# A hybrid decoder step on one core: every SBUF row set to begin at a multiple of 256 bytes

## The chip, the core and the metric

The kernel runs on 1 core of one Trainium2 chip. The metric is the device time of one execution in microseconds, as a median over runs. A core has four computing engines with their own instruction queues (TensorE, called PE; VectorE, DVE; ScalarE, ACT; GpSimd, POOL), a fifth queue that mostly issues transfers (SyncE, SP), and 16 DMA engines. Its working memory, SBUF, has 128 partitions, and a "row" below is a stretch of consecutive bytes within one partition.

## The reference

One inference step of one decoder layer, for a prompt of 1,024 tokens and for 8 samples of 4 tokens (32 columns), in float32. Cut to what matters:

```python
h, gate = adaln_in(x, c, w_ada, b_ada, g_norm)       # RMS norm, scaled and shifted by a projection of c
(mq, mk, mv, mi, mf, mo, mz, aq, ak, av, az, gm, ga) = split_in(h @ w_in)
y_m, C, n, m = mlstm_branch(...)                     # 4 heads of 128, in chunks of 128 tokens, with a carried state
o = attn_prompt(q, k, v, sinks)                      # 8 query heads of 64, window 128, a sink per head
y_a = o * silu(az)
u = sigmoid(gm) * (y_m @ w_mo) + sigmoid(ga) * (y_a @ w_ao)
x = x + gate * (u @ w_o)
y = rmsnorm(x, g_final)
```

Outputs are y for prompt and samples, the mLSTM state, and the keys and values that are kept.

## The kernel before

**Layout.** Activations lie transposed: a partition is a channel (modulo 128), a column a token. T = 1,056 columns are the 1,024 prompt tokens and the 32 sample columns. Every float32 operand of a large product is split into two float32r tiles, a rounded high part and the remainder; a product is the sum of three matmuls, high by high, high weight by low moving, low weight by high moving. In the names, `h_h` and `h_l` are the two parts of h, and `wh_...` and `wl_...` those of the weights. In the trace's `out<-moving,weight` the moving operand comes first.

**Memory.** SBUF tiles come from two pools, `cp` for constants (each tile for the whole kernel) and then `sp` for working tiles. In `sp` each tag has a fixed number of slots, and a new tile of a tag takes a slot that an earlier one has left; whoever first writes it waits for the last reader of the earlier one. The tags that matter:

- `half` (helper `ht`): 50 slots of 128x512 float32, 2,048 bytes a partition. Nearly everything passes through it: raw x, attention units (`uqv`, `ukv`, `p`), mLSTM loads (`hq`, `hk`, `hv`, `et`, `qw`), gates (`gt`, `tga`), sums for a Strassen scheme (`t2h0` and so on) and the split output weights (`wo_...`).
- `wr` (9 slots), `wh` and `wl` (4 each): weights of 128x4x128, also 2,048 bytes.
- `h0`, `h1`, `l0`, `l1`: one slot each, the four large tiles. Each holds four rows of T columns (4,224 bytes): `h_h0` has channels blocks 0 to 3 of the high part, `h_h1` 4 to 7, `h_l0` and `h_l1` the remainders. Before that the same slots hold weights (`early_...`), later the high and low parts of the mLSTM output (`ym_h0`, `ym_l0`), the merged branches (`u_h1`, `u_l1`) and output rows (`rows_h`, `rows_l`).

As the built program places them, the pools' first tile begins at byte 1,152. The first `half` slot begins at byte 16,928, the `wr` slots at 119,328, `h0` at 137,760, `h1` at 154,656, `l1` at 171,552, `wh` at 188,704, `wl` at 196,896 and `l0` at 205,088. All of these leave the remainder 32 when divided by 256. A row of a large tile is 16.5 times 256 bytes, so its rows 0 and 2 leave the remainder 32 too, and its rows 1 and 3 the remainder 160.

**Stages.** Condition projections and the norm of x (about 0 to 65 us); the first projections `g_ak`, `g_av`, then `g_aq`, `g_mq`, `g_mk`, `g_mv` in pieces of 384, 384 and 288 columns that read rows of `h_h` and `h_l` (to about 215 us); 18 pairs of projections by a Strassen scheme (`block_products`: seven products `bx`, `bw`, `by`, `bz` of 12 matmuls of 512 columns per pair), of which four read rows of the large tiles (b11, b21, b22, t1) and three read sums in `half` slots (t2, t3, t4) (to about 650 us); the attention output by the same scheme; the mLSTM output (`g_w_mo`, pieces of 384, 384 and 288 columns that read rows of `ym`); the output product (`foX`, `foW`, `foY`, `foZ`) whose operands all lie in `half`, `wr`, `wh` and `wl` slots, and the final norm.

**Order.** PE's instructions stand in the order in which they are written out; a planner (`Side`) drops attention units, mLSTM head stages and the output-weight preparation (`out_weights`) between them by estimated times. In the middle of the kernel DVE, ACT and SP are ordered by the framework's scheduler, which knows the slots. A weight is split (`split_ahead`, a cast on ACT and a subtraction on DVE) two products before its use.

Of the kernel before, what the change touches and what calls it, by code (L numbers as in the profile page):

```python
# [10 lines left out]
F32 = mybir.dt.float32  # L11
F32R = mybir.dt.float32r
# [11 lines left out]
NT = 4  # L24
NS = NB * NT
T = SEQ + NS
NH = 4
PAST = 8192
WIN = 128
# [5 lines left out]

C_ID, C_S9, C_TRI, C_CM, C_AM, C_TS, C_CS, C_RS, C_S32, C_BM, C_S64 = 0, 128, 137, 265, 393, 649, 681, 713, 745, 777, 785
C_END = 849


def shape_constants():  # L40
    f = np.float32
    c = np.zeros((128, C_END), f)
    i = np.arange(128)
# [8 lines left out]
    c[:NS, C_CS:C_CS + NS] = np.where(ok, 0, NEG)  # L52
    c[:NH, C_RS:C_RS + NS] = np.where(s % NT == 0, NEG, 0)[None]
    for r in range(9):
# [9 lines left out]
    cs, sn = np.cos(ang).astype(f), np.sin(ang).astype(f)  # L64
    rope = np.zeros((128, 2, T), f)
    rope[:, 0] = 1
# [15 lines left out]
def job_columns():  # L82
# [5 lines left out]
    for g in range(4):  # L88
        cols["aq", g] = aq + pair(g)
        cols["az", g] = az + pair(g)  # L90
    for h in range(NH):
        for n, s in (("mq", mq), ("mk", mk), ("mv", mv), ("mo", mo), ("mz", mz)):
# [80 lines left out]
def body(tc, a):  # L173
    nc = tc.nc
    with ExitStack() as ctx:
        cp = ctx.enter_context(tc.tile_pool(name="cp", bufs=1))
        sp = ctx.enter_context(tc.tile_pool(name="sp", bufs=1))
# [3 lines left out]
        def pg(shape, name):  # L181
            return ps.tile(shape, F32, tag="g", bufs=2, name=name)
# [8 lines left out]
            return ps.tile(shape, F32, tag="o", bufs=2, name=name)  # L191

        def ht(shape, name, dt=F32):
            return sp.tile(shape, dt, tag="half", bufs=50, name=name)

        def sm(shape, name, bufs=3, dt=F32):
            return sp.tile(shape, dt, tag=name, bufs=bufs, name=name)
# [43 lines left out]
        def dma(out, in_, late=False):  # L241
            stores(in_.tensor)
            issue(out, in_, late)
# [52 lines left out]
        def load_x(p, k0, k1, ts):  # L296
            for k in range(k0, k1):
                ts.append(ht([128, 512], f"x{p}_{k}"))
                dma(ts[-1], a["xT"][:, p, k])
# [4 lines left out]
        issue(small, a["small"])  # L304
        load_x(0, 2, KT, xT[0])
        load_x(1, 0, KT, xT[1])
        cst = cp.tile([128, C_END], F32, name="cst")
        vec = cp.tile([128, 28], F32, name="vec")
        cT, xS = (small[:, o:o + KT * n].rearrange("p (k n) -> p k n", k=KT) for o, n in ((C_TRI + 28, 9), (C_TRI + 28 + KT * 9, NS)))
# [21 lines left out]
        def quarter(x, shape, name, dt=F32):  # L331
            return sp.tile(shape, dt, tag=x, bufs=1, name=f"{name}_{x}")
# [46 lines left out]

        hD = dp.tile([128, KT, T], F32, name="hD")  # L380
        PARTS = (0, 512), (512, 512), (SEQ, NS)
# [143 lines left out]
        hs = {}  # L525

        def h_hi(k, c0, n, x="h"):
            ks = k
            if isinstance(k, slice):
                k, ks = k.start, slice(k.start % 4, (k.stop - 1) % 4 + 1)  # L530
            q = f"{x}{k // 4}"
            if q not in hs:
                hs[q] = quarter(q, [128, 4, T], "h", F32R)
            return hs[q][:, k % 4 if k is ks else ks, c0:c0 + n]

        h_lo = lambda k, c0, n: h_hi(k, c0, n, "l")
# [58 lines left out]
        def gates(gp, zg, bias):  # L595
# [43 lines left out]
            nm, wi = gt2[:, 0], gt2[:, 1]  # L639
            aTs = cp.tile([NH, NS], F32, name="aTs")  # L640
            bTs = cp.tile([NH, NS], F32, name="bTs")
            V.tensor_copy(aT, tp[:32, 0])
# [56 lines left out]

            m0 = cp.tile([NH, NB], F32, name="m0")  # L700
            dma(m0, a["m0T"])
            cms = cp.tile([NH, NS], F32, name="cms")
            V.tensor_tensor_scan(cms, cst[:NH, C_RS:C_RS + NS], aTs, NEG, ALU.add, ALU.max)
# [107 lines left out]
        osm = cp.tile([128, NH, NS], F32, name="osm")  # L811
        yaD = [dp.tile([128, T], F32, name=f"yaD{g}") for g in range(4)]

# [157 lines left out]
        yhD = [dp.tile([128, SEQ], F32, name=f"yhD{h}") for h in range(NH)]  # L971
        ymD = [dp.tile([128, T], F32, name=f"ymD{h}") for h in range(NH)]
        qs = cp.tile([128, NH, NS], F32, name="qs")
# [274 lines left out]
        def split(src, his, los, cols, k, eng=V):  # L1248
            for i, c in enumerate(cols):
                raw = ht([128, 512], "yr")[:, :c.stop - c.start]  # L1250
                dma(raw, src[k][:, c])
                hi, lo = his(k, c.start, c.stop - c.start), los(k, c.start, c.stop - c.start)
                S.copy(hi, raw)
                eng.tensor_tensor(lo, raw, hi.bitcast(F32), op=ALU.subtract)

        PCOLS = [slice(c0, c0 + n) for c0, n in PIECES]
        HALF = slice(0, 512), slice(512, SEQ)
        taD, tmD = ([dp.tile([128, T], F32, name=f"{n}{d}") for d in range(KT)] for n in ("taD", "tmD"))

# [313 lines left out]
        ut, ymt = [], []  # L1573
        u = lambda k, c0, n: ut[k // 4][:, k % 4, c0:c0 + n]
# [96 lines left out]
        def att_products():  # L1671
            jobs = [AttPair(i) for i in range(4)]
            flat = [(0, 1)]
            for n in range(4):
                flat += [(n, i) for i in (5, 6, 2, 7)] + ([(n + 1, 1)] if n < 3 else []) + [(n, 3), (n, 4)]

            def split_ahead(j):
                if j < len(flat):
                    jobs[flat[j][0]].split(flat[j][1])

            yield
            ymt.extend(quarter(x, [128, 4, T], "ym", F32R) for x in ("l0", "h0"))
            yield
            jobs[0].load()
            for k in range(4):
                dma(c32[:, k], yaD[k][:, SEQ:T])
            yield
            jobs[0].gates()
            yield
            yield  # L1690
            jobs[0].split(1)
            jobs[0].samples()
            jobs[0].first_sums()
            yield
            jobs[0].split(5)
            yield
            ut.extend(quarter(x, [128, 4, T], "u") for x in ("h1", "l1"))
            for j, (n, i) in enumerate(flat):
                job_ = jobs[n]
                nxt = jobs[n + 1] if n < 3 else None  # L1700
                if i == 1 and nxt:
                    nxt.load()
                if i == 6:
                    if nxt:
                        nxt.gates()
                    if n in (0, 1, 3):
                        split(ymD, *ymx, PCOLS, {0: 2, 1: 3, 3: 1}[n], G if n == 3 else V)
                if i == 3 and n == 2:
                    split(ymD, *ymx, PCOLS, 0)
                if i == 2 and not nxt:  # L1710
                    for d in range(2):
                        preload(("w_mo", d))
                split_ahead(j + 2)
                if i == 3 and not nxt:
                    prefetch(("w_mo", 0))
                    gated(("w_mo", 0))
                if i == 1:
                    o = NX = pg([128, 512], "ax")
                elif i == 5:
                    o = Z = pa([128, 512], "az")  # L1720
                else:
                    o = {2: lambda: X, 3: lambda: W, 4: lambda: Y, 6: lambda: W, 7: lambda: Y}[i]()
                new = i in (1, 5)
                wh, wl = job_.w.pop(i)
                for k in range(2):
                    side.until(lambda: k in ya[OPERANDS[i]])
                    bh, bl = ya[OPERANDS[i]][k]
                    mm(o, wh[:, k], bh, start=(new and k == 0), stop=False, more=not new)
                    mm(o, wh[:, k], bl, start=False, stop=False, more=not new)
                    mm(o, wl[:, k], bh, start=False, stop=(k == 1), more=not new)  # L1730
                    side.tick()

                def copy_of(pool, name, src):
                    t = pool([128, 512], name)
                    if n == 0 and (j == 0 or i == 6):
                        mm(t, job_.g["A"][0][:, 0], ya["b11"][0][0], start=True, stop=True)
                    S.copy(t, src)
                    return t

                if i == 6:  # L1740
                    Y = copy_of(pa, "ay", W)
                    job_.samples_end()
                elif i == 2:
                    job_.done(0, 0, X)
                    if nxt:
                        nxt.samples()
                        nxt.first_sums()
                elif i == 5:
                    p5 = ht([128, 512], "p5")
                    S.copy(p5, Z)  # L1750
                elif i == 7:
                    job_.done(1, 1, p5, Y)
                elif i == 3:
                    job_.done(0, 1, p5, W)
                elif i == 4:
                    job_.done(1, 0, Y)
                if j == 0 or (i == 3 and nxt):
                    X = NX
                    W = copy_of(pg, "aw", X)
# [421 lines left out]
        for i, r in enumerate(blocks_of_rows):  # L2181
# [65 lines left out]
            else:  # L2247
# [9 lines left out]
                for f, (y, (c0, n)) in enumerate(zip(Y, parts)):  # L2257
# [3 lines left out]
                    if f:  # L2261
                        V.tensor_tensor(xb[1][:, hi], xb[1][:, hi], gf[:, hi], op=ALU.mult)
                        half = norm_sum(ss[:, 2:4], 1, 2)
# [82 lines left out]
```

## Time and profile before

| | |
|---|---|
| median of 3 runs | 842.34 us (842.21 to 842.41) |
| the profiled execution: its time | 842.49 us |
| its span, first to last instruction | 840.7 us |
| granted TensorE clock, mean | 0.997 |
| PE busy | 819.6 us (97%), 5,129 matmuls |
| DVE busy | 599.2 us (71%) |
| ACT busy | 421.7 us (50%) |
| POOL busy | 66.2 us (8%) |
| moved by DMA | 153.96 MB, 183 GB/s over the span |

Times inside the span count from its start. Matmuls overlap, so the length of one matmul in the trace is more than what it adds; what it adds is read from start to start. A line of the chain of waits such as `12.3 2.77 PE by L258 x12` says that twelve matmuls in a row took 2.77 us of the path that ended last. All recorded operations of DVE and ACT carry line 219 and all matmuls line 258, those of helpers.

### The profile page before, as it was taken

Reading aid. Unit: us, or ns where it says so; the run is one execution under the profiler, and the core shown is the slowest. Engines: PE = TensorE matmul, PEld = TensorE weight load, DVE = VectorE, ACT = ScalarE, POOL = GpSimd, SP = SyncE. Lnnn points to the kernel's source line nnn. Section 1 sums busy time; section 2 is a strip of 40 time slices with the busy share of each in tenths; the row PEclk is TensorE's granted clock in tenths of the full one; section 3 lists DMA queues with packets and bytes.
Section 4 is the critical chain, followed back from the end, with each engine's and each line's share of the span. In section 5 each row is a group of like instructions: output and inputs, shape, how many; then the busy total and the mean of one; then the engine's idle time right before and its main releaser. Section 6 shows DMA issues by size and latency. Waiting matters only on the chain.

```text
span 840.7 us, 15062 instructions
## 1 busy us (share of the span) xinstructions
PE 819.6 (97%) x5129; PEld 666.8 (79%) x5129; DVE 599.2 (71%) x1501; ACT 421.7 (50%) x1032; POOL 66.2 (8%) x128
## 2 busy tenths in 40 slices
PE   6999999999999999999999999999999999999996
PEld 3779897888788788887788877777777779997775
DVE  4889886656655555656657776787878988974776
ACT  5664365655475464445464545344545654334342
POOL 0120000000000000000000100000002104250000
PEclk9999999999999999999999999999999999999998
DMA  9997756356445333579735433553345685643532
GB/s 334 374 355 232 201 184 202 117 155 210 138 135 170 104 115 93 179 247 321 261 131 186 139 124 118 166 177 127 126 149 189 210 288 183 205 138 127 200 108 106
DMA packets 106690, 153.96 MB, mean 183 GB/s; under 512 B 20449, under 2 KB 54369, under 8 KB 106581
## 3 DMA queue, kind: packets, MB, share of 16 engines
q1 hardware_dynamic: 100964, 142.25, 51.9%
q10 hardware_dynamic: 4176, 6.56, 2.2%
q0 software_dynamic: 1472, 4.20, 1.3%
q8 instruction: 40, 0.66, 0.3%
q14 instruction: 38, 0.30, 0.1%
HBM read 109.22 MB, written 44.75 MB: 183 GB/s over the span
## 4 chain that ended last, share of the span: by engine, by line
PE 88%; DMA 5%; DVE 4%; issue 1%; ACT 1%; SPq 0%; DVEq 0%; ACTq 0%
PE bw L258 11%; PE bx L258 11%; PE by L258 10%; PE g_aq L258 6%; PE g_w_mo L258 6%; PE bz L258 5%; PE g_mq L258 3%; PE foW L258 3%; PE foX L258 3%; PE foY L258 2%; PE sc L258 2%; PE oT L258 2%; PE foZ L258 2%; PE smp L258 2%; PE pt L263 2%; PE n L258 2%
## 5 line engine op out<-in xcount | busy, mean ns | idle before, releaser
L219 ACT ACTIVATE p<-p,nmx 128x256 f32<-128x256 f32 (+1 forms) x64 | 31.0, 485 | 10.6 <-DVE nmx L219 10.3
L258 PE MATMUL g_aq<-h_h,wh_aq 128*128 128x384 f32 (+1 forms) x96 | 32.5, 338 | 0.0
L219 DVE CUSTOM_DVE_ANT_0 p<-sc,cst,sink 128x256 f32<-128x256 f32 (+1 forms) x64 | 26.2, 464 | 8.3 <-PE sc L258 8.2
L258 PE MATMUL g_w_mo<-ym_l,wh_w_mo 128*128 128x384 f32 (+1 forms) x96 | 31.1, 324 | 0.0
L258 PE MATMUL g_aq<-h_l,wh_aq 128*128 128x384 f32 (+1 forms) x96 | 31.0, 323 | 0.0
L258 PE MATMUL g_w_mo<-ym_l,wl_w_mo 128*128 128x384 f32 (+1 forms) x96 | 31.0, 323 | 0.0
L258 PE MATMUL g_aq<-h_h,wl_aq 128*128 128x384 f32 (+1 forms) x96 | 31.0, 323 | 0.0
L258 PE MATMUL g_w_mo<-ym_h,wh_w_mo 128*128 128x384 f32 (+1 forms) x96 | 31.0, 323 | 0.0
L246 POOL DMA_DIRECT2D oD<-uqv x16 | 8.8, 552 | 202.5 <-ACT uqv L219 172.8
L219 ACT ACTIVATE et<-et,an 128x128 f32<-128x128 f32 x32 | 11.2, 395 | 25.7 <-DVE et L219 21.3
L258 PEld LDWEIGHTS g_aq<-h_h,wh_aq 128*128 128x128 f32 x96 | 18.1, 188 | 2.6 <-issue 1.5
L219 DVE COPY p<-pt 128x512 f32<-128x512 f32 (+1 forms) x16 | 10.5, 655 | 12.3 <-PE pt L263 12.3
L258 PE MATMUL sc<-ukv,uqv 64*128 64x256 f32 (+1 forms) x128 | 18.3, 390 | 0.8 <-DVE p L219 0.8
L258 PEld LDWEIGHTS g_aq<-h_l,wh_aq 128*128 128x128 f32 x96 | 18.1, 188 | 0.0
L258 PEld LDWEIGHTS g_w_mo<-ym_h,wh_w_mo 128*128 128x128 f32 x96 | 18.0, 188 | 0.0
L258 PEld LDWEIGHTS g_w_mo<-ym_l,wh_w_mo 128*128 128x128 f32 x96 | 18.0, 188 | 0.0
L219 ACT ACTIVATE p<-p,den 128x256 f32<-128x256 f32 (+1 forms) x32 | 14.4, 491 | 7.3 <-DVE den L219 7.3
L258 PEld LDWEIGHTS g_aq<-h_h,wl_aq 128*128 128x128 f32 x96 | 18.0, 188 | 0.0
L258 PEld LDWEIGHTS g_w_mo<-ym_l,wl_w_mo 128*128 128x128 f32 x96 | 18.0, 188 | 0.0
L219 DVE TENSOR_TENSOR wor<-wor,gb 128x512 f32<-128x512 f32 x16 | 10.8, 690 | 9.8 <-DMA wor<-w_out 9.7
L258 PE MATMUL g_mq<-h_h,wh_mq 128*128 128x384 f32 (+1 forms) x48 | 16.9, 351 | 0.3 <-ACT mk L219 0.3
L219 ACT ACTIVATE sq<-rows_h 128x512 f32<-128x512 f32 (+2 forms) x14 | 8.2, 583 | 17.8 <-issue 12.0
(2078 smaller groups left out, 2858.7 us busy)
## 6 DMA issues: line engine op xcount, KB each, us to landing
x<-xT SPq DMA_DIRECT2D x16, 256.0 KB, 5.4
early_h<-w_ada SPq DMA_DIRECT2D x8, 512.0 KB, 9.0
adar_ga<-w_ada SPq DMA_DIRECT2D x16, 256.0 KB, 4.3
wr_ga<-w SPq DMA_DIRECT2D x16, 256.0 KB, 2.9
wr_gm<-w SPq DMA_DIRECT2D x16, 256.0 KB, 3.5
taD<-gt SPq DMA_DIRECT2D x16, 256.0 KB, 2.0
tmD<-gt SPq DMA_DIRECT2D x16, 256.0 KB, 4.4
wor<-w_out SPq DMA_DIRECT2D x16, 256.0 KB, 6.6
```

What stands on the lines that cost most here:

```text
L219: ins = f(*args, **kw)
L246: ins = (eng or nc.sync).dma_start(out, in_)
L258: in_order(nc.tensor.matmul(out, lhsT, rhs, start=start, stop=stop, skip_group_check=more))
L263: in_order(nc.tensor.transpose(out, in_, idn))
```

## The change

A tile of 56 float32 (224 bytes) is taken first from the constants' pool and never used, so that everything behind it moves up by 224 bytes. The four large tiles get rows of 1,088 columns in place of 1,056 in three of their uses (h, ym, u), of which the last 32 are never touched. The `half` tag goes from 50 slots to 49. In the built program `half` then begins at byte 17,152, `wr` at 117,504, `h0` at 135,936, `h1` at 153,344, `l1` at 170,752 and `wh` at 188,416, all multiples of 256, and a row of a large tile is 17 times 256 bytes. No operation of the computation is added or removed. PE's and POOL's instructions keep their order; the scheduler places some of the others differently.

```diff
+PITCH = 1088
...
+LEAD = 56
...
         def ht(shape, name, dt=F32):
-            return sp.tile(shape, dt, tag="half", bufs=50, name=name)
+            return sp.tile(shape, dt, tag="half", bufs=49, name=name)
...
         load_x(1, 0, KT, xT[1])
+        cp.tile([128, LEAD], F32, name="lead")
         cst = cp.tile([128, C_END], F32, name="cst")
...
             if q not in hs:
-                hs[q] = quarter(q, [128, 4, T], "h", F32R)
+                hs[q] = quarter(q, [128, 4, PITCH], "h", F32R)
...
-            ymt.extend(quarter(x, [128, 4, T], "ym", F32R) for x in ("l0", "h0"))
+            ymt.extend(quarter(x, [128, 4, PITCH], "ym", F32R) for x in ("l0", "h0"))
...
-            ut.extend(quarter(x, [128, 4, T], "u") for x in ("h1", "l1"))
+            ut.extend(quarter(x, [128, 4, PITCH], "u") for x in ("h1", "l1"))
```

## The prediction

> **What bounds the kernel now.** The page first, then the busy time by stage, the chain of waits, and single matmuls in the timeline.
>
> ```profile
> span 840.7 us, 15062 instructions
> PE 819.6 (97%) x5129; PEld 666.8 (79%) x5129; DVE 599.2 (71%) x1501; ACT 421.7 (50%) x1032; POOL 66.2 (8%) x128
> ...
> PE 88%; DMA 5%; DVE 4%; issue 1%; ACT 1%; SPq 0%; DVEq 0%; ACTq 0%
> ```
> ```profile
> 0.00:21.00 21.00, 13.92 (x82) 6.31 (x84) 10.13 (x39) 10.88 (x19) 0.53 (x5) 1.00 0.92 334
> 21.00:65.00 44.00, 43.19 (x315) 33.00 (x309) 37.26 (x85) 28.99 (x50) 6.96 (x12) 1.00 1.01 361
> ...
> 300.00:400.00 100.00, 98.95 (x632) 81.23 (x632) 60.01 (x141) 48.09 (x123) 4.75 (x12) 1.00 0.60 198
> ...
> 699.00:746.00 47.00, 47.00 (x292) 46.87 (x291) 41.20 (x68) 14.72 (x27) 16.28 (x12) 1.00 0.54 170
> 746.00:830.00 84.00, 84.00 (x393) 66.13 (x392) 56.02 (x118) 37.56 (x93) 6.09 (x5) 1.00 0.45 154
> 830.00:841.00 11.00, 3.19 (x27) 2.98 (x25) 5.70 (x16) 2.16 (x6) 0.00 (x0) 0.78 0.25 96
> ```
>
> From about 21 to 830 us PE is never idle for long (1.05 us of 100 between 300 and 400), at full clock. So what the change does to the step from one matmul to the next counts in full, and what it does to transfers counts only where PE stands: in the first 21 us (7.1 us without PE) and in a few short gaps. The profiled execution took 842.49 us, 0.15 above the median of 842.34; I sum against it and take 0.15 off at the end.
>
> **Steps between matmuls, and what a row's start has to do with them.** The chain of waits has two kinds of products of 512 columns:
>
> ```profile
> 388.97 2.77 PE by L258 x12
> 404.81 2.77 PE bw L258 x12
> ...
> 793.41 4.08 PE foX L258 x18
> 804.16 4.08 PE foW L258 x18
> ```
>
> 4.08 us for 18 is 226.7 ns a matmul, 2.77 for 12 is 230.8. In the output product (`foX`, `foW`) every operand lies in a slot with remainder 32. In the Strassen stage four products of seven walk through rows of `h_h` and `h_l`, whose remainders change between 32 and 160 after every three matmuls. The same stage has clean stretches too, until a product on `h` rows starts:
>
> ```profile
> 380.11 0.39 PE L258 MATMUL bw<-t2h,wh_pgate__4499 128*128 128x512 f32 x1
> ...
> 381.92 0.39 PE L258 MATMUL bw<-t2h,wl_pgate__4500 128*128 128x512 f32 x1
> 382.15 0.33 PE L258 MATMUL smpo<-cst,smps 128*128 128x64 f32 x2
> ...
> 382.60 0.40 PE L258 MATMUL bx<-h_l,wh_pgate__4529 128*128 128x512 f32 x1
> ...
> 383.99 0.40 PE L258 MATMUL bx<-h_l,wh_pgate__4529 128*128 128x512 f32 x1
> ```
>
> From 380.11 to 381.92 are 8 steps of 226 ns, from 382.60 to 383.99 are 6 of 232. But the small `smpo` lies between, and small matmuls upset the rhythm too. The pieces of 384 columns separate the causes, since they pass through four rows of one tile without anything between:
>
> ```profile
> 26.32 0.34 PE L258 MATMUL g_ak<-h_h,wh_ak 128*128 128x384 f32 x1
> 26.49 0.34 PE L258 MATMUL g_av<-h_h,wh_av 128*128 128x384 f32 x1
> ...
> 742.83 0.34 PE L258 MATMUL g_w_mo<-ym_l,wh_w_mo 128*128 128x384 f32 x1
> 743.00 0.34 PE L258 MATMUL g_w_mo<-ym_h,wh_w_mo 128*128 128x384 f32 x1
> ...
> 743.35 0.34 PE L258 MATMUL g_w_mo<-ym_l,wh_w_mo 128*128 128x384 f32 x1
> 743.53 0.34 PE L258 MATMUL g_w_mo<-ym_h,wh_w_mo 128*128 128x384 f32 x1
> ```
>
> A first matmul on a row of remainder 160 that follows a row of 32 holds PE for 180.0 ns on average (96 such, from 26.32 to 743.35), a first one on a row of 32 after 160 for 174.0 (77 such, the last at 742.83). Six nanoseconds for the same columns, weights of the same form and the same place in the triple speak for the address.
>
> Sum of this part. For 512 columns: 18 pairs of 7 products are 126 products of 12, and 2.77 − 12 × 0.2267 = 0.05 us each gives 6.3 us that could go. The matmuls of other work between the products upset the rhythm whatever the address, and it comes back only within some ten matmuls, so I take half: −3.0 us, with ends 0 and −6.3. For 384 columns: 672 such matmuls, in groups of three with 180.0, and about 175 for the other two, against 174.0, where half of the groups enter an odd row: (6 + 2 × 1) / 3 × 336 = 0.9 us: −0.9, ends 0 and −1.7. The pieces of 288 columns step evenly:
>
> ```profile
> 87.74 0.29 PE L258 MATMUL g_aq<-h_h,wl_aq 128*128 128x288 f32 x1
> ...
> 90.67 0.34 PE L258 MATMUL g_aq<-h_h,wh_aq 128*128 128x384 f32 x1
> ```
>
> 22 steps in 2.93 us are 133.2 ns; I count nothing.
>
> A rule that speaks against this: the Trainium skill, "SBUF — State Buffer", section "Specifications (TRN2)", says that SBUF has lines of 16 bytes and that crossing to a new line costs. 32 and 160 are both multiples of 16, so by it the two kinds of rows read alike, this part is worth 0 and the sum below ends at 842.1. The 180.0 against 174.0 do not agree with that.
>
> **One slot fewer.** With 49 slots the tiles of `half` fall on other slots. For each of the 620 reuses I compared, in the trace of before, when the slot's new predecessor was last read with when the tile was first written. Before, no tile is early, as must be; with the new slots 31 of them come too early, by 5.6 us at most. Most are loads that are wanted much later:
>
> ```profile
> 174.94 0.32 SPq L246 DMA_DIRECT2D hv<-vD  x1
> 180.61 0.32 SPq L246 DMA_DIRECT2D et<-nmd  x1
> ...
> 203.52 0.49 PE L263 MATMUL tv<-cst,hv 128*128 128x128 f32 x3
> ```
>
> This `hv` is the worst, 5.6 us late, so at 180.6. Behind it on SP stands only `et`, which goes at 180.61 anyhow, and PE reads `hv` at 203.52: nothing. Two places matter, both while `out_weights` fills the slots. First ACT:
>
> ```profile
> 402.07 0.57 ACT L219 ACTIVATE gt<-by 128x512 f32<-128x512 f32 x1
> ...
> 405.20 0.58 ACT L219 COPY p<-bz 128x512 f32<-128x512 f32 x1
> 407.44 0.62 ACT L219 CAST wh_pgate__4946<-wr_ga 128x512 fp32r<-128x512 f32 x1 [1.66 <-issue]
> ```
>
> The copy at 405.20 gets the slot of the `gt` of 402.07, which must first be stored. In the new order that store stands ahead of a `wor` load on SP, near 402.7; with the 4.4 us to landing below it is done near 407.1. ACT stands until then, and behind it the cast of 407.44, which comes some 0.3 us late. ACT's idle 1.66 us covers the rest; without it the whole 1.9 us would fall on a cast that is made two products (5.5 us) ahead.
>
> ```profile
> tmD<-gt SPq DMA_DIRECT2D x16, 256.0 KB, 4.4
> ```
>
> Second, the longest wait of PE in the middle:
>
> ```profile
> 414.84 0.32 SPq L246 DMA_DIRECT2D et<-nmd  x1
> 415.27 0.36 SPq L246 DMA_DIRECT2D wr_gm<-w  x1
> 418.90 0.56 DVE L219 TENSOR_TENSOR et<-et,cst 128x384 f32<-128x384 f32 x1 [2.47 <-DMA et<-nmd]
> 419.38 0.34 DVE L219 SCALAR_TENSOR_TENSOR C<-C,dec,U 128x129 f32<-128x129 f32 x1
> ...
> 419.77 0.71 PE L258 MATMUL S<-hq,hk 128*128 128x128 f32 x4 [1.40 <-DVE C L219]
> ```
>
> DVE waits 2.47 us for the load of `et`, `C` stands behind it, and PE waits 1.40 us for `C`. With the new slots this load would go 2.9 us later; but in the order of the changed program DVE has `C` ahead of `et`, behind the sum over `wr_gm`, whose load comes earlier by one place. Then `C` would be done near 418.5 in place of 419.7, and what is late next is the exponentials of `et` on ACT. I take −0.8, with ends −1.4 (the wait gone) and +1.5 (2.9 late, less what the new order gives). For the 29 other tiles I take +0.6, with ends 0 and +3.
>
> **Transfers.** The first load and the x tiles:
>
> ```profile
> 1.65 4.26 DMA small<-small
> ```
> ```profile
> x<-xT SPq DMA_DIRECT2D x16, 256.0 KB, 5.4
> ```
>
> In the first 21 us the DMA engines are 92% busy and PE lacks 7.1 us, most of it before the first load has landed. Shorter packets could give some of that, not their fixed part. I take −0.2, ends 0 and −0.7 (a tenth of the 7.1). The Trainium skill, "DMA: Bandwidth & Descriptors", section "How a descriptor splits into AXI transactions", says that a descriptor which starts off a multiple of 256 bytes has its first transaction at the boundary below it. By it a packet of 2,048 bytes at remainder 32 takes 9 transactions and 65 beats, and 8 and 64 after; an estimate from that is 1.5% of the transfer time, 0.3 us of 21. No row here shows an aligned packet beside the others.
>
> **Sum.** −3.0 − 0.9 − 0.8 + 0.6 − 0.2 = −4.3: 842.49 − 4.3 = 838.2, and 838.0 as a median.
>
> **The rivals.**
>
> *Nothing on PE (0.17).* The six nanoseconds come from something else that goes with the row, or DVE and ACT, no faster than before, hold PE back at new places. For it: the rows of `h` also differ in their distance to the weights' slots. Against it: waits on PE are few, so there is slack to use up. Time: 842.3 − 0.8 + 0.6 − 0.2 = 841.9.
>
> *Slower through the lost slot (0.18).* PE gains nothing or little, and at 395 to 425 us the stores that free slots hold ACT and DVE in order: the copy at 405 by up to 3.2 us if its store lands as late as before, a sum on DVE just behind it by 2.6, the load of `et` by 2.9. From the point where a weight's split comes more than about 4.2 us late (5.5 us of two products less 1.3 for cast and subtraction) PE stands. Two such places at about 1.5 us and no gain give 845.3. For it: DVE is the fullest of the other engines, at 71%. Against it: the scheduler's new order puts the waiting ones back.
>
> *The constant part goes (0.03).* Between 288 and 512 columns the step grows by 93.5 ns for 224 columns, 0.417 each; so 226.7 holds 13 ns that do not depend on the columns. Were these the price of a start at remainder 32, some 3,000 matmuls would save up to 40 us: 803. Against it: 13 ns is there after a row of 160 and of 32 alike. The Trainium skill, "TensorE: Matmul & The Clock Gate", section "Wait — 56ns, not 53.3ns?", gives only about 2.5 ns for that part, for another data type; by it the time would be near 810.
>
> That the change doesn't do what it says can be left out: the built program has the addresses.
>
> **How the numbers follow.** A measurement of this kernel can tell about 0.2%, 1.7 us. The forecast (0.62) is 838.0; its own range is 833.5 to 840.6, from the ends of the two matmul terms and the wait. The rival of nothing lies within 1.7 us for the most part, the third is far below. The range that I give, 833.0 to 845.0, leaves out the third case, the upper half of the slower one and the tails. Faster: 0.62 + 0.03 = 0.65; same 0.17; slower 0.18.
>
> **What would show it.** Right: products of 12 in the chain at 2.72 to 2.74 us where nothing lies between them; first matmuls on rows 1 and 3 of 384 columns at 174 ns; `S` at about 418 without its wait of 1.40; `tv` at the same place in the order with no wait for `hv`. Wrong: those steps unchanged at 180 and 2.77, or unchanged total with new waits of PE on ACT or DVE between 395 and 425 us.

## The result, and the profile after

The changed kernel takes 835.76 us (median of 4 runs, 834.12 to 836.09) against 842.38 before (842.21 to 844.59, 4 runs): a ratio of 0.9913, 95% interval 0.9894 to 0.9932, or 6.6 us. It was run again in three of the comparisons below, at 836.66, 836.23 and 835.79, with ratios of 0.9927, 0.9920 and 0.9926. The forecast was 838.0, the range 833.0 to 845.0. The profiled execution after took 835.73 us. Its page:

```profile
span 833.9 us, 15075 instructions
PE 813.9 (98%) x5129; PEld 665.7 (80%) x5129; DVE 597.2 (72%) x1501; ACT 421.7 (51%) x1032; POOL 67.0 (8%) x128
```

The same 5,129 matmuls keep PE busy for 5.7 us less. In the timeline of PE, a pair of products on rows of `h` with nothing between them, first as it was before, then after:

```profile
391.58 0.39 PE L258 MATMUL bx<-h_h,wh_pgate__4599 128*128 128x512 f32 x1
...
394.34 0.39 PE L258 MATMUL bw<-h_h,wh_pgate__4679 128*128 128x512 f32 x1
```
```profile
388.95 0.39 PE L260 MATMUL bx<-h_h,wh_pgate__4600 128*128 128x512 f32 x1
...
391.67 0.39 PE L260 MATMUL bw<-h_h,wh_pgate__4680 128*128 128x512 f32 x1
```

Twelve matmuls of 512 columns take 2.76 us before and 2.72 after, that is 230 and 226.7 ns a step. The pieces of 384 columns that were quoted at 743 us before now go evenly over the four rows, seven steps of 173 ns:

```profile
735.88 0.33 PE L260 MATMUL g_w_mo<-ym_l,wl_w_mo 128*128 128x384 f32 x1
...
737.09 0.33 PE L260 MATMUL g_w_mo<-ym_l,wh_w_mo 128*128 128x384 f32 x1
```

From start to start, over all pairs of matmuls of the same width that follow one another (steps under 260 ns):

| columns | steps before, after | mean before | mean after | gain |
|---|---|---|---|---|
| 512 | 1,783, 1,785 | 230.08 ns | 228.47 ns | 2.9 us |
| 384 | 589, 589 | 176.25 ns | 174.61 ns | 1.0 us |
| 288 | 308, 308 | 136.42 ns | 135.48 ns | 0.3 us |

That is 4.1 us, gained little by little between 25 and 750 us. Of the 2.9 us, 1.8 came in the products on rows of `h` (231.19 to 228.80 ns a step) and 0.9 in the three products of sums in `half` slots (230.33 to 228.73 ns), whose operands agreed before and after. The rest came in jumps, at waits. PE's waits after:

```profile
PE xc L260 <- ACT xsq L221: 7.1, 1, 7.1
PE sc L260 <- DVE p L221: 1.2, 1, 1.2
...
PE S L260 <- DVE C L221: 0.4, 1, 0.4
```

`S` waits 0.4 us in place of 1.40. A wait of 0.78 us for `wor` at 379 us is gone in this execution. One before `sc` grew from 0.8 to 1.2. The first load landed 0.7 us later, which was made up by 25 us.

### The profile page after: what moved, and what is told of

Read it like the earlier page. It is cut to its first block, busy times and chain, and to the rows that moved or that the text cites. A ratio compares the mean times of both kernels' runs of the same rounds, so it can differ in the third digit from the quotient of the medians.

```text
span 833.9 us, 15075 instructions
## 1 busy us (share of the span) xinstructions
PE 813.9 (98%) x5129; PEld 665.7 (80%) x5129; DVE 597.2 (72%) x1501; ACT 421.7 (51%) x1032; POOL 67.0 (8%) x128
```

## Experiments

The scheduler gives the kernels with 49 slots one order of instructions, and those with 50 slots another. So kernels of the same number of slots differ in addresses alone.

**One part of the change at a time.** `e1_pitch_only` has the 49 slots and the rows of 1,088, without the lead; `e2_lead_only` has the lead, without the others; `e3_slots49` has 49 slots alone.

Against the changed kernel `e1_pitch_only` has

```diff
-        cp.tile([128, LEAD], F32, name="lead")
```

and against the kernel before `e2_lead_only` and `e3_slots49` have

```diff
+        cp.tile([128, LEAD], F32, name="lead")
```
```diff
-            return sp.tile(shape, dt, tag="half", bufs=50, name=name)
+            return sp.tile(shape, dt, tag="half", bufs=49, name=name)
```

> Rows of 1,088 columns and 49 slots, but no lead: every row, slot and weight leaves the same remainder 32, none begins at a multiple of 256 bytes. All instructions stand in the order of the changed kernel. Theory (a change of the remainder from one moving row to the next breaks the pace of the matmuls; the remainder itself costs nothing): as the changed kernel, 835 to 837 us; first matmuls of 384 columns all near 174 ns, steps of 512 columns 228.5 on average as against 230.1 before. Rival (rows must begin at a multiple of 256 bytes): only what the new order gives, 840 to 841.5 us, 512 columns at 230 or more.

> The lead alone: 50 slots, rows of 1,056 columns, all instructions in the order of the kernel before. All slots and rows 0 and 2 of the large tiles begin at a multiple of 256 bytes, rows 1 and 3 leave 128. Theory (change of the remainder): 842.4 us as before, within 1 us, 384 columns at about 180 ns on entering an odd row. Rival (a multiple of 256 counts): the 1,300 matmuls on slots and even rows gain some 1.3 ns each, about 840.5 us. Rival (transfers gain by whole beginnings): the start and the loads are shorter, 841.5 to 842 us, and packets of 2,048 bytes take less than the 84 ns of before.

> 49 slots alone: addresses behind the slots move by 2,048 bytes, remainders 32 and 160 as before, all instructions in the order of the changed kernel. Theory: only the changed waits of the new order, which in the trace after give 1.0 us less before S, 0.8 less before a bw, and 0.5 more before an sc: 841 us, from 840.3 to 842. Rival (the order and the slots bring the gain): 836 us. Rival (a lost slot costs, covered by the rows' gain): 843 us or more.

| kernel | rows / weights leave | us (runs) | ratio to before (842.96), 95% |
|---|---|---|---|
| pitch only | 32 / 32 | 836.87 (6) | 0.9931 (0.9916 to 0.9946) |
| lead only | 0 and 128 / 0 | 842.64 (12) | 1.0001 (0.9984 to 1.0018) |
| 49 slots | 32 and 160 / 32 | 839.50 (5) | 0.9964 (0.9951 to 0.9976) |

The lead gives nothing: neither does it help alone, nor is it missed. Without it no row begins at a multiple of 256 bytes, and the same products step as in the changed kernel:

```profile
392.75 0.39 PE L259 MATMUL bx<-h_h,wh_pgate__4599 128*128 128x512 f32 x1
...
395.47 0.39 PE L259 MATMUL bw<-h_h,wh_pgate__4679 128*128 128x512 f32 x1
```

2.72 us again. Over the whole span the starts of matmuls in the two traces differ only by jumps at waits and by some slow steps behind one of them. The transfers show no gain at the median either: a packet of 2,048 bytes takes 84 ns in the traces of before, of lead only and of the changed kernel. And 49 slots alone are already faster than before by 3.5 us, where I had expected 841.

**What about the row's start?** A probe without the rest of the kernel: 48 matmuls of 512 columns in a row, weights at remainder 0.

> Leaves the whole computation out: series of 48 matmuls of 512 columns alone (zeros, four weights in turn), one PSUM tile each, every series twice (the second time in reverse order). r0, r32, r128, r16, r4: all moving rows begin at that remainder of 256. s0_128 and so on: the beginning changes between the two remainders after every three matmuls; a0_128, a0_256 after every one. Theory: r0, r32, r128, r16 step at 226.7 ns; s0_128 and s32_160 at 230 to 231; s0_256 and s32_288 at 226.7. For r4, s0_64, s0_32, s0_16, s0_4 the trace of before says nothing: if any change of the remainder breaks the pace, all of the s at 229 to 232. Rival (only a multiple of 256 is free): r32, r128, r16, r4 at 230 or more. Rival (neither, the pace is lost to other engines and small matmuls): all series at 226.7.

The mean of the last 24 steps of each series, worked out from the starts in the trace (both passes of a series agree to 0.3 ns):

```
r0       226.7    s0_128   232.3    s0_64   232.8
r32      233.3    s32_160  234.4    s0_32   231.1
r128     232.2    s0_256   226.7    s0_16   232.0
r16      231.7    s32_288  233.3    s0_4    231.7
r4       236.7    a0_128   230.0    a0_256  226.7
```

Here rows of 32 are slow although nothing changes, while in `e1_pitch_only` they are fast. In the probe the weights left 0, in that kernel 32. So a new theory: what counts is that moving rows and weights leave the same remainder (a row that does is said to agree with the weights below). Two tests, one in the kernel (pads of 128 bytes ahead of `wh` and of `l0`, moving rows as in the changed kernel) and one in a second probe:

```diff
+            if tag == "wh":
+                pad("padw")
             return sp.tile([128, 4, 128], dt, tag=tag, bufs=bufs, name=name)
...
+            if x == "l0":
+                pad("padl")
             return sp.tile(shape, dt, tag=x, bufs=1, name=f"{name}_{x}")
```

> The changed kernel with a pad of 128 bytes ahead of the wh slots and one ahead of l0: every moving row still begins at a multiple of 256 bytes and never changes its remainder, but the stationary weights in wh and wl leave 128. All instructions stand in the order of the changed kernel. Theory A (a change of the remainder from one moving row to the next breaks the pace): nothing changes, 835 to 837 us. Theory B (the pace is kept where the moving row and the weights leave the same remainder; in the first probe the weights left 0, and moving rows of 128 stepped at 232.2 ns, of 0 at 226.7): nearly all large products mismatch; some 2,000 steps of 512 columns at 232 in place of 228.5 and 670 of 384 columns some 4 ns longer, 845 to 849 us, slower than the kernel before, in which only about half of the matmuls mismatch.

> The changed kernel itself on the same chip as the run above, for the comparison. Both theories: 835 to 837 us.

> Leaves the whole computation out: series of 48 matmuls alone as in the first probe, now with the remainder of the weights (w) and of the moving rows (m) set apart; s32_160 changes after every three; n384, n288, n256 have that many columns; small_ has a small plain float32 matmul after every 12. Theory A (change of the moving row): w0_m0, w32_m32, w128_m128, w32_m0, w128_m0, w0_m128 all at 226.7 ns, which the first probe speaks against. Theory B (equal remainders of weights and moving rows): w0_m0, w32_m32, w128_m128, w16_m16, w4_m4 at 226.7; w32_m0, w128_m0, w0_m128, w32_m160, w0_m64 at 230 to 234; w32_s32_160 at 231 to 233 and w32_s32_288 at 226.7; n384 at 173.3 against 177 to 179. Theory C (only moving rows at a multiple of 256 are free): w32_m32, w128_m128 at 232 to 233, w32_m0 and w128_m0 at 226.7. For small_m0 all theories: between 227 and 230, since the steps after a small matmul are longer for some ten matmuls in the kernel.

| kernel | us (runs) | ratio to before (842.81), 95% |
|---|---|---|
| weights at 128 | 844.38 (12) | 1.0025 (1.0012 to 1.0038) |
| changed kernel | 836.66 (6) | 0.9927 (0.9908 to 0.9947) |

With every row at a multiple of 256 bytes, and the weights beside it by 128, the kernel is 7.7 us slower than the changed one, and slower than before. Theory A has fallen, and theory C falls with the second probe's `w32_m32` below. The same two products:

```profile
391.99 0.40 PE L260 MATMUL bx<-h_h,wh_pgate__4602 128*128 128x512 f32 x1
...
394.79 0.40 PE L260 MATMUL bw<-h_h,wh_pgate__4682 128*128 128x512 f32 x1
```

2.80 us, 233 ns a step; on average over 1,786 steps of 512 columns 232.4 against 228.5, of 384 columns 176.5 against 174.6. The time is 0.6 us under the range that I gave. Four stretches of the second probe's timeline, each within one series and holding 43 to 47 of its 48 matmuls (start, length, count; the last one's own 0.4 us is to be taken off before dividing by the count less one). Weights 0 and rows 0, 32 and 32, then 4 and 4, then 32 and 0:

```profile
27.05 10.82 PE L212 MATMUL w_m<-mov,wgt 128*128 128x512 f32 x47
37.94 10.61 PE L212 MATMUL w_m<-mov,wgt 128*128 128x512 f32 x46
...
70.87 10.39 PE L212 MATMUL w_m<-mov,wgt 128*128 128x512 f32 x43
82.28 10.42 PE L212 MATMUL w_m<-mov,wgt 128*128 128x512 f32 x44
```

These are 227, 227, 238 and 233 ns. By the last 24 steps: `w0_m0`, `w32_m32`, `w128_m128` and `w32_s32_288` 226.7; `w32_m0`, `w128_m0`, `w0_m128`, `w32_m160` 232.1 to 233.3; `w32_s32_160` 232.2. Theory B holds at 0, 32 and 128, and fails for small remainders: `w16_m16` 231.1, `w4_m4` 237.8. `w0_m64` had 228.9 in one pass and 233.3 in the other. For 384 columns equal remainders give 173.3, 0 against 128 gives 176 (I had expected 177 to 179), and a change after every three 175.6. For 288 columns it is 131.7 against 133.3, and for 256 the other way round, 120.0 against 118.6, so the rule does not hold for every width. In `small_m0`, expected at 227 to 230, the steps behind a small matmul have a mean of 231 ns, the first one, of 314, left out.

**How many rows disagree.** The last test of the theory was one of its size, on the same chip with the kernel of 49 slots and the changed one:

```diff
-PITCH = 1088
+PITCH = 1072
```

> 49 slots, no lead, rows of 1,072 columns: rows of the large tiles leave 32, 224, 160 and 96, so only one row in four agrees with the weights (32), as against two in four with rows of 1,056. All instructions stand in the order of the changed kernel. Theory B (equal remainders of weights and moving rows keep the pace): 672 in place of 456 of the 2,022 matmuls of 512 columns disagree, 504 in place of 336 of those of 384; at the 4.4 ns above 226.7 and 173.3 that such ones show in the trace of before, and the more upset steps behind them, 1 to 1.7 us longer than the kernel with 49 slots alone of the same chip, so 841 to 842. Rival (the longer row itself, with space behind its end, is what helps): as with 1,088, 836 to 837 us.

> 49 slots alone once more, with the two others of this call on one chip: what the new order gives, apart from the rows. Traces: 1.5 us less than before from the waits at 378 and 418 us and the start, so 840 to 841.5; the first run's times: 839.5.

> The changed kernel on the same chip: 4.5 us below the kernel with 49 slots alone, if the rows give what the two traces show from 25 to 750 us (step for step, without the waits); 835 to 837.

| kernel | us (runs) | ratio to before (842.89), 95% |
|---|---|---|
| rows of 1,072 | 840.16 (12) | 0.9974 (0.9960 to 0.9988) |
| 49 slots | 840.34 (12) | 0.9967 (0.9957 to 0.9978) |
| changed kernel | 836.23 (6) | 0.9920 (0.9904 to 0.9936) |

The longer row by itself does not help, so that rival is out. But three disagreeing rows of four cost no more than two of four, and my 1 to 1.7 us were wrong. I had multiplied the matmuls that disagree by a price. In the trace of rows of 1,072 steps of 512 columns have a mean of 230.1 ns, as with 49 slots alone. Where rows change after every three matmuls, the agreeing ones lose the pace too: in the trace of before, steps on rows of `h` at 32 took 231.5 ns on average (370 of them), those on rows at 160 230.8 (340). Behind an upset the even pace comes back only after six to ten agreeing steps in the second probe, and three give nothing. How far rows and weights differ matters too, and not alike for all widths. In the trace of rows of 1,072, steps of 384 columns take 173.3 ns on rows at 192 from the weights, 174.9 at 64 and 178.1 at 128, where agreeing rows take 174.3; with 512 columns the rows at 192 are the slowest, 233.1 against 230.3 to 230.8 for the others.

So the rows give 836.23 − 840.34 = −4.1 us, the sum of the steps above, and the new order gives −2.6. The first three kernels, with only 5 and 6 runs behind the difference, share it out otherwise: 836.87 − 839.50 = −2.6 for the rows and −3.5 for the order. I go by the second set, which the steps bear out.

**What is late at 416 us.** In the four traces of the changed kernel `S` waited 0.4, 2.7, 1.4 and 0.5 us for `C`. DVE in the trace of `e6_after_again`:

```profile
417.43 0.69 DVE L221 TENSOR_TENSOR ws<-wr_gm,wr_gm 128x512 f32<-128x512 f32 x1 [3.63 <-DMA wr_gm<-w]
418.04 0.35 DVE L221 SCALAR_TENSOR_TENSOR C<-C,dec,U 128x129 f32<-128x129 f32 x1
```

`C` stands behind a sum that waits for a load. One exchange in DVE's order, and nothing else, tests it:

```diff
+                        if not p:
+                            lastC[:] = [getattr(c_ins, "ins", c_ins)]
...
+                if self.name == "gate5":
+                    no_sync(getattr(s_ins, "ins", s_ins), lastC)
```

> The changed kernel with two operations of DVE exchanged: the third C of the last head's first group now stands ahead of the sum ws over wr_gm of the gate pair 5, everything else in the same order. In three traces of the changed kernel PE's S at about 416 us waited 0.4, 1.4 and 2.7 us for this C, which stood behind ws, and ws waited for the load of wr_gm. Theory (the load of wr_gm in front of C is what is late): S has no wait, or one under 0.3 us, in the trace; 834.5 to 835.8 us as a median, 0.5 to 1.5 below the changed kernel of the same chip, and no runs above 837.5, since a wait of about 2 us or more is followed by seven or eight matmuls at 427 in place of 227 ns. Rival (something else is late at the same time, such as the load of et or hk): S waits as long, 836 to 837.

> The changed kernel on the same chip, for the comparison: 835.5 to 837, S waiting 0.4 to 2.7 us for C.

834.74 us (6 runs, 834.38 to 837.45) against 835.79 (6 runs, 834.50 to 839.64) for the changed kernel of the same chip, 0.9916 (0.9903 to 0.9930) and 0.9926 (0.9909 to 0.9942) of before. Their intervals overlap, so the 1.05 us are not beyond doubt; that the wait goes is:

```profile
413.95 0.35 DVE L221 SCALAR_TENSOR_TENSOR C<-C,dec,U 128x129 f32<-128x129 f32 x1 [0.63 <-PE n L260]
414.58 0.69 DVE L221 TENSOR_TENSOR ws<-wr_gm,wr_gm 128x512 f32<-128x512 f32 x1 [0.28 <-DMA wr_gm<-w]
```

`S` is not among PE's waits in this trace. It has the lowest median of all the kernels here.

## Why the prediction was right, step by step

- **512 and 384 columns, −3.0 and −0.9.** Measured −2.9 and −1.0. First matmuls on rows 1 and 3 went from 180.0 to 173.9 ns (96 of them), as named. The half of 6.3 was a guess, and it came out: before, the 1,783 steps stood 6.1 us above 226.7 ns each, and 2.9 of that went. Its reason holds as well: the second probe has a series with a small float32 matmul after every twelve, and its steps at equal remainders come back to 227 only after six to nine. All seven products of a pair were counted, though only four read rows of `h`; that held because the other three start in the upset which those leave. The output product, which agreed before, kept its pace (227.45 and 227.42 ns).
- **288 columns, 0.** Measured −0.3. I read 22 even steps of 133.2 ns and took that for no loss. By the second probe 133.3 is the pace of rows that disagree by 128, and 131.7 that of agreeing ones.
- **Why the rows matter.** The step said that rows of remainder 160 are read more slowly than those of 32. As worded this is wrong: rows are slow where they leave another remainder than the weights, or where agreeing and disagreeing ones alternate. It gave the right number because the weights happened to leave 32, and the change worked because it moved rows and weights to the same remainder; that part was luck. Why the two starts must agree stays open, and so do the small remainders and the narrow widths, where the rule fails. The rule of 16-byte lines from the Trainium skill, "SBUF — State Buffer", section "Specifications (TRN2)", gives no price for any of these series, all multiples of 16 but the ones with 4. The runs do not agree: 226.7 against 233.3.
- **`S` at 418, −0.8.** In the two traces −1.0, by the step foreseen, `C` ahead of `et`. What is late next was wrong: not the exponentials, but `ws` and its load. And the size is that of one execution. This, with the next term, is the part of the sum that failed: together −0.2 for the new order, while the kernels of 49 and of 50 slots on one chip differ by 2.6 us. I took the 1.40 us of the one trace as the most that could be won there (−1.4). With the same order of instructions, DVE in the trace of `e2_lead_only` (an execution of 849.24 us, the longest of its kernel) has

```profile
423.69 0.56 DVE L220 TENSOR_TENSOR et<-et,cst 128x384 f32<-128x384 f32 x1 [6.39 <-DMA et<-nmd]
424.16 0.35 DVE L220 SCALAR_TENSOR_TENSOR C<-C,dec,U 128x129 f32<-128x129 f32 x1
```

  and PE waits 5.33 us for `C`. In the nine traces of the 49 slots' order without the last exchange the same wait is between nothing and 2.71 us, 0.9 on average. A load that lands late holds `C` back in either order: in the old one that of `et`, in the new one that of `wr_gm`, which there goes out 2.6 to 4.8 us ahead of `et`.
- **Other late tiles, +0.6.** Not seen as a loss. The wait for `wor` at 379 us,

```profile
379.31 0.50 PE L258 MATMUL bw<-t2h,wh_pgate__4499 128*128 128x512 f32 x1 [0.78 <-DVE wor L219]
```

  gave 0.95 us in the two traces, with the longer steps behind it, though SP, whose loads it hangs on, has the same order there. It is 0.78 and 0.42 in the two traces of the old order, and in the ten of the new one nothing in seven and 0.20, 0.74 and 0.41 in the others. The wait before `sc` went the other way: 0.76 and 1.14 in the old order, 1.2 on average in the new. With two traces of the old order it is not settled how the 2.6 us are shared among these waits in an average execution.
- **Transfers, −0.2.** Nothing to be seen in the time: lead only is at 1.0001. In the first 21 us packets of 2,048 bytes take 90.1 to 92.7 ns on average in the seven traces with slots at a multiple of 256, and 91.2 to 93.0 in the five with slots at 32. The 1.5% that I estimated from the Trainium skill, "DMA: Bandwidth & Descriptors", section "How a descriptor splits into AXI transactions", would be 1.4 ns; the means of the two groups differ by 1.1 ns, but they overlap, so these runs neither show it nor rule it out.
- **The sum.** −4.3 was forecast, −6.6 measured: each row term right to 0.3 us, the order off by 2.4. The forecast's own range, 833.5 to 840.6, is not what its ends add up to: with the two matmul terms and the wait at their ends, and the rest as forecast, they give 833.3 to 844.2.
- **Rivals.** Nothing on PE: refuted by the steps. But what was said for it, that the rows of `h` differ in their distance to the weights' slots, is closer to what the probes showed than the step that was forecast. Slower through the lost slot: the copy on ACT did wait for its store (0.97 us) and its cast was not late for PE; the order was a gain. The constant 13 ns: still in every step of 226.7.

## What to carry to other kernels

Give the moving rows and the stationary weights of float32r matmuls the same start modulo 256 bytes, and keep it along a run of matmuls; the common remainder may be 32 or 128 as well as 0, so a pitch may do and no lead is needed. This was seen with 288, 384 and 512 columns; with 256 columns it was not, and remainders of 16 and 4 were slow even where they agree. Judge a stage by whether its steps ever reach the even pace (226.7 ns here), not by counting the ones that are off. When slots change, compare the orders of the queues for what comes earlier too, and price the order by a kernel that changes nothing else.

## What was not expected of the hardware

A wait of PE can cost more than itself. After the 2.71 us before `S` in `e6_after_again`, PE's granted clock in the stretches that follow is (stretch, length, PE busy and count, clock, share of DMA, GB/s):

```profile
418.40:419.60 1.20, 1.16 (x7) 0.98 0.62 85
419.60:422.80 3.20, 3.20 (x10) 0.50 0.29 97
422.80:425.00 2.20, 2.20 (x11) 0.96 0.31 119
```

```profile
419.79 0.63 PE L260 MATMUL bx<-h_h,wh_pgate__4881 128*128 128x512 f32 x1
420.21 0.63 PE L260 MATMUL bx<-h_l,wh_pgate__4881 128*128 128x512 f32 x1
```

In the clock records of this trace 0.50 lasts 3.41 us, and the steps of 427 ns in it add 1.6 us on top of the wait. The same 3.41 us and 1.6 us followed waits of 1.72 us (before `sc`, `e12_after_fourth`) and 1.88 (before `sc`, `e1_pitch_only`); with the wait of 5.33 (before `S`, `e2_lead_only`) it was 6.83 us and some 2.2 us. Eight waits of 1.17 to 1.40 us in six traces had no such steps behind them. The Trainium skill, "TensorE: Matmul & The Clock Gate", section "HAM oscillation — how this bites in real kernels", has the rule that gaps should not exceed about 3.4 us; here 1.72 was enough.

The records tell more. In all twelve traces of whole kernels the granted clock, once it is full, changes only after a whole number of stretches of 3.41 us (after 82 to 242 of them the first time). Every such stretch in which PE did nothing for 1.71 us or more was followed by 0.50, and every one with 1.64 us or less by full clock. So in these traces the idle time within one stretch decides, with the limit at about half of it. Where a wait falls should then matter too, but no trace here has a wait of over 1.71 us that two stretches share so that neither reaches it. This goes with the scatter of a kernel's runs (834 to 840 us for the changed one), since the two waits, before `sc` and `S`, differ from execution to execution; how much of the scatter it makes is not shown, as only one execution of each run has a trace.
